# Eight pairs of activation tiles at eight different byte offsets from the weights, modulo 256

## The chip, the core and the metric

The kernel runs on one core of one Trainium2 chip. The metric is the time of one execution on the device, in microseconds (us); the median of the runs shown is compared. TensorE (PE in the profile) does the matrix products, VectorE (DVE), ScalarE (ACT) and GpSimd (POOL) the rest. PEld is TensorE's load of the stationary operand, which the profile lists apart from the matmul that uses it. SP and ACT issue the transfers from memory.

## What is computed

Two layers over x of 512 tokens and 1024 channels, in float32. Each normalises, projects, mixes and projects back onto a residual:

```python
def pool_mixer(h, w_in, w_grp, scale, w_out):
    v, gate = jnp.split(h @ w_in, 2, axis=-1)                 # 1024 -> 2 x 2048
    p = multiscale_pool(v)                                    # trailing means minus the token
    m = jnp.einsum('btgc,gcd->btgd', p, w_grp).reshape(B, T, D_INNER) * scale
    return (m * jax.nn.silu(gate)) @ w_out

def hgrn2_mixer(h, w_in, lb, norm_g, w_out):
    q, fz, i, gate = jnp.split(h @ w_in, 4, axis=-1)          # 1024 -> 4 x 2048
    ...                                                       # gated recurrence in chunks -> o
    return (o * jax.nn.silu(gate)) @ w_out

def reference(x, ...):
    h = x
    h = h + pool_mixer(rms_norm(h, norm_g[0]), ...)
    h = h + hgrn2_mixer(rms_norm(h, norm_g[1]), ...)
    return rms_norm(h, final_g)
```

## The kernel before

**Products in three passes.** A float32 operand is split into a high part and the rest, both of the type fp32r, by `split` (lines 93 to 95; ScalarE casts the high part on line 94, VectorE subtracts on line 95). `mm3` (lines 125 to 128) makes each 128 x 128 by 128 x 512 product from three matmuls: high weights with high activations (line 126), high with low (127), low with high (128). In `matmul(out, a, b)` the operand a is stationary (128 columns are loaded into the array) and b is moving (512 columns stream through it). Each of the three matmuls loads its stationary operand afresh.

**What is stationary and what moves.** `piece` (line 97) loads 512 KB of weights into a tile `wraw` and splits it into `whi` and `wlo` (six buffers each); SP issues the loads, 300 places ahead. `scaled_halves` (line 197) writes the eight pairs `xh0, xl0 .. xh7, xl7`, one for each 128 channels of the normalised input, once in each layer. The products are:

- x moving, weights stationary (`project4` and `project`, lines 130 to 149): the values and gates of layer 0, and the forget, query and gate projections of layer 1. 640 products, 1920 matmuls. The loop over the eight pairs k is outside the three matmuls, and in `project4`, the first projection of each layer, outside four outputs as well.
- x stationary, weights moving (`inputs`, line 394): 128 products, 384 matmuls.
- layer 0, `ph`/`pl` and `zh`/`zl` moving, weights stationary (`mixed` and `project_out`): 64 and 128 products, 192 and 384 matmuls.
- layer 1, `z1h`/`z1l` stationary, weights moving (`out_half`, first three groups): 96 products, 288 matmuls; for the last group `zz` (high part in the slot of `kk`, low part in that of `q`): 32 products, 96 matmuls.

Together 3264 matmuls of 512 columns. The other 774 matmul records are short ones of the recurrence, of transposes and of sums.

**Where the tiles lie.** Within a partition, the scratch of the program comes first, then the pools one behind the other in the order of lines 68 to 71 (`const`, `wpool`, `act`, `small`), then the pool of the layer (`l0`, then `l1` in its place). Within a pool, tiles lie in the order of their first creation, each from a multiple of 32 bytes. A tile whose size is a multiple of 256 bytes leaves the phase (the address modulo 256) as it was; the odd sizes move it. By these sizes:

| tiles | phase before | off the weights |
|---|---|---|
| `wraw`, `whi`, `wlo` | 128 | 0 |
| `xh0 .. xl7` (2048 bytes each) | 128 | 0 |
| `ph`, `pl`, `zh`, `zl` (behind two `win` tiles of 2112 bytes) | 0 | 128 |
| `kk`: high part of `zz` (behind `first`, 2 x 32 bytes) | 192 | 64 |
| `q`: low part of `zz` (behind `e`, 2 x 32 bytes more) | 0 | 128 |
| `z1h`, `z1l` (behind `mo` and `ro`, 128 bytes more) | 128 | 0 |

Slices of a weights tile start at multiples of 512 bytes, so the table holds for every slice.

Of the kernel before, what the change touches and what calls it, by code (L numbers as in the profile page):

```python
# [32 lines left out]
F32 = mybir.dt.float32  # L33
# [7 lines left out]
P = 128  # L41
# [3 lines left out]
KD = D // P  # L45
# [5 lines left out]
EPS = 1e-6  # L51
WINDOWS = (2, 4, 8, 16)
RAW, WB = 3, 6
WARM = 10
NORM_AT, SPREAD_AT = (KD - 2, 2), (KD - 1, 1)
AHEAD = 300
# [9 lines left out]
def trunk(ctx: ExitStack, tc: tile.TileContext, xT, par, ident_d, causal_d, mask_d, fg_d, w0_in, w0_grp, w0_out, w1_in, w1_out, out):  # L66
    nc = tc.nc
    const = ctx.enter_context(tc.tile_pool(name="const", bufs=1))
    wpool = ctx.enter_context(tc.tile_pool(name="wpool", bufs=1))
    act = ctx.enter_context(tc.tile_pool(name="act", bufs=1))  # L70
# [9 lines left out]
    warm = pa.tile([P, 512], F32, name="a", tag="a", bufs=4)  # L80
    for _ in range(WARM):
        nc.tensor.matmul(warm[:, :P], ones, ones, start=True, stop=True)
# [3 lines left out]
    nc.scalar.dma_start(out=pp, in_=par)  # L86
    ident = const.tile([P, P], F32, name="ident")
    mhalf = const.tile([P, 8], F32, name="mhalf")
    nc.gpsimd.memset(mhalf, -0.5)

    h = [const.tile([P, T], F32, name=f"h{k}") for k in range(KD)]
# [99 lines left out]
    def spread_sbuf(rn):  # L191
# [2 lines left out]
        nc.scalar.copy(out=rb, in_=spread(rn))  # L194
        return rb

    def scaled_halves(k, col):
        g = pp[:, col + k:col + k + 1]
        hi = act.tile([P, T], F32R, name=f"xh{k}", tag=f"xh{k}", bufs=1)
        lo = act.tile([P, T], F32R, name=f"xl{k}", tag=f"xl{k}", bufs=1)  # L200
        nc.scalar.activation(out=hi, in_=h[k], func=AF.Copy, scale=g)
        nc.vector.scalar_tensor_tensor(out=lo, in0=h[k], scalar=g, in1=hi, op0=ALU.mult, op1=ALU.subtract)
        return hi, lo
# [13 lines left out]
    with tc.tile_pool(name="l0", bufs=1) as l0:  # L217
        xs, pieces = [], []
        wv = w0_in.rearrange("(k p) n -> p k n", p=P)
        for i in range(4):  # L220
            raw = wpool.tile([P, 2, GC], F32, name="wraw", tag="wraw", bufs=RAW)
            hi = wpool.tile([P, 2, GC], F32R, name="whi", tag="whi", bufs=WB)
            lo = wpool.tile([P, 2, GC], F32R, name="wlo", tag="wlo", bufs=WB)
            for j in range(2):
                k = 2 * i + j
                nc.sync.dma_start(out=h[k], in_=xT[k * P:(k + 1) * P, :])
                nc.sync.dma_start(out=raw[:, j], in_=wv[:, k, 0:GC])
                xs.append(scaled_halves(k, C_NG0))
                split(raw[:, j], hi[:, j], lo[:, j])
                pieces.append((hi[:, j], lo[:, j]))  # L230
# [90 lines left out]
    def hgrn(ctx, general):  # L321
# [6 lines left out]
        for a in Ads:  # L328
            nc.gpsimd.memset(a, 0.0)

        xs = [scaled_halves(k, C_NG1) for k in range(KD)]
        accs, rn, rb = project4(load_in(w1_in, DI), xs, lambda: rms(f"l1{name}", h))

# [447 lines left out]
```

## Time and profile before

| | |
|---|---|
| median of 2 runs | 842.99 us (842.31 to 843.68) |
| the profiled execution: its own time | 843.0 us |
| the profiled execution: span from first to last instruction | 841.2 us |
| PE busy | 826.4 us, 98% of the span |
| DVE, ACT, POOL busy | 550.9, 275.2, 160.6 us |
| mean DMA rate | 94 GB/s |

The profile gives for each engine the time in which an instruction of it was under way. Successive matmuls overlap in it: each is listed for about 0.39 us, and the next starts long before that is over. So neither the busy share nor the listed duration tells how fast the products go; the distance from the start of one matmul to the start of the next does, and the timeline gives the starts.

### The profile page before, as it was taken

To read this page: it belongs to the slowest core of one execution; us is meant where nothing else is said; L and a number is where in the kernel's file an instruction comes from. 1 tells how busy PE (TensorE), PEld (TensorE's weight loads), DVE (VectorE), ACT (ScalarE), POOL (GpSimd) and SP (SyncE) were. 2 spreads that over 40 slices of the span, in tenths; PEclk is the share of its full clock that TensorE was granted. 3 is DMA by queue.
4 is the path that set the end of the run, shared out by engine and by line. 5 is a ranking of instruction groups with operands and counts; after the bars stand their busy time and mean duration, and the time that the engine had idled before them with its cause. 6 is when DMAs were issued, how large, how long until landed. Compare 5 with 4: busy or idle time off the path is not lost.

```text
span 841.2 us, 10459 instructions
## 1 busy us (share of the span) xinstructions
PE 826.4 (98%) x4038; PEld 684.8 (81%) x4038; DVE 550.9 (65%) x837; ACT 275.2 (33%) x474; POOL 160.6 (19%) x204
## 2 busy tenths in 40 slices
PE   9899999999999999999999999999999999999995
PEld 7688888888888888888888888888888888888884
DVE  7766645753686456699269974459974459973744
ACT  7342224213323145323433240433240433242311
POOL 4020001001002013071223300213300213302100
PEclk9999999999999999999999999999999999999998
DMA  6622323122422245223032240332240333230202
GB/s 218 213 75 77 100 101 101 53 98 101 150 82 97 75 151 175 76 76 125 1 101 79 71 141 10 101 101 87 80 135 1 101 101 92 82 128 1 101 13 91
DMA packets 37194, 79.06 MB, mean 94 GB/s; under 512 B 2832, under 2 KB 3088, under 8 KB 37136
## 3 DMA queue, kind: packets, MB, share of 16 engines
q1 hardware_dynamic: 34688, 74.46, 27.1%
q10 hardware_dynamic: 2448, 3.86, 1.3%
q8 instruction: 33, 0.54, 0.3%
q14 instruction: 25, 0.20, 0.1%
HBM read 74.11 MB, written 4.19 MB: 93 GB/s over the span
## 4 chain that ended last, share of the span: by engine, by line
PE 95%; DVE 1%; DMA 1%; ACT 1%; issue 0%; POOL 0%; SPq 0%; POOLq 0%; DVEq 0%; ACTq 0%
PE mm L126 29%; PE mm L127 29%; PE mm L128 29%; PE a L556 2%; PE a L594 2%; PE a L574 1%; PE a L596 1%; PE a L563 1%; DMA wraw<-in_w0i 1%; PE a L438 1%; DVE wlo L95 1%; DMA h<-in_xT 0%; PE a L342 0%; ACT whi L94 0%; PE a L188 0%
## 5 line engine op out<-in xcount | busy, mean ns | idle before, releaser
L126 PE MATMUL mm<-xh,whi 128*128 128x512 f32 x640 | 251.2, 393 | 1.3 <-ACT whi L94 0.7
L128 PE MATMUL mm<-xh,wlo 128*128 128x512 f32 x640 | 249.7, 391 | 1.0 <-DVE wlo L95 1.0
L127 PE MATMUL mm<-xl,whi 128*128 128x512 f32 x640 | 249.7, 390 | 0.0
L94 ACT CAST whi<-wraw 128x1024 fp32r<-128x1024 f32 (+1 forms) x140 | 141.9, 1025 | 252.3 <-PE mm L127 115.5
L95 DVE TENSOR_TENSOR wlo<-wraw,whi 128x1024 fp32r<-128x1024 f32 (+1 forms) x140 | 172.7, 1261 | 57.6 <-ACT whi L94 56.6
L126 PEld LDWEIGHTS mm<-xh,whi 128*128 128x128 f32 x640 | 120.6, 188 | 27.1 <-ACT whi L94 1.4
L128 PEld LDWEIGHTS mm<-xh,wlo 128*128 128x128 f32 x640 | 120.4, 188 | 27.2 <-DVE wlo L95 2.0
L127 PEld LDWEIGHTS mm<-xl,whi 128*128 128x128 f32 x640 | 120.5, 188 | 24.5
L541 DVE RECIPROCAL r<-r 128x512 f32<-128x512 f32 x16 | 53.4, 3340 | 1.5 <-POOL r L540 1.5
L128 PE MATMUL mm<-zh,wlo 128*128 128x512 f32 x128 | 50.6, 395 | 0.0
L126 PE MATMUL mm<-zh,whi 128*128 128x512 f32 x128 | 50.6, 395 | 0.0
L127 PE MATMUL mm<-zl,whi 128*128 128x512 f32 x128 | 50.5, 395 | 0.0
L126 PE MATMUL mm<-whi,xh 128*128 128x512 f32 x128 | 50.1, 391 | 0.0
L128 PE MATMUL mm<-whi,xl 128*128 128x512 f32 x128 | 49.9, 390 | 0.0
L127 PE MATMUL mm<-wlo,xh 128*128 128x512 f32 x128 | 49.9, 390 | 0.0
L351 DVE TENSOR_TENSOR ht<-mm,ht 128x512 f32<-128x512 f32 x32 | 22.1, 689 | 35.5 <-PE mm L128 35.5
L214 DVE TENSOR_TENSOR h<-mm,h 128x512 f32<-128x512 f32 x32 | 22.0, 689 | 32.4 <-PE mm L128 32.3
L414 POOL TENSOR_TENSOR gs<-fz,s 128x512 f32<-128x512 f32 x16 | 21.4, 1336 | 98.6 <-ACT s L412 98.6
L272 POOL TENSOR_TENSOR gs<-gt,sg 128x512 f32<-128x512 f32 x16 | 21.3, 1330 | 92.4 <-ACT sg L270 92.3
L126 PE MATMUL mm<-whi,z1h 128*128 128x512 f32 x96 | 37.6, 392 | 0.0
L128 PE MATMUL mm<-whi,z1l 128*128 128x512 f32 x96 | 37.4, 389 | 0.0
L127 PE MATMUL mm<-wlo,z1h 128*128 128x512 f32 x96 | 37.4, 389 | 0.0
(141 smaller groups left out, 1164.9 us busy)
## 6 DMA issues: line engine op xcount, KB each, us to landing
wraw<-in_w1i SPq DMA_DIRECT2D x64, 512.0 KB, 3.9
wraw<-in_w0i SPq DMA_DIRECT2D x28, 512.0 KB, 4.2
wraw<-in_w0o SPq DMA_DIRECT2D x16, 512.0 KB, 3.9
wraw<-in_w1o SPq DMA_DIRECT2D x16, 512.0 KB, 4.3
wraw<-in_w0g SPq DMA_DIRECT2D x8, 512.0 KB, 4.1
h<-in_xT SPq DMA_DIRECT2D x8, 256.0 KB, 5.0
wraw<-in_w0i SPq DMA_DIRECT2D x8, 256.0 KB, 5.2
hmid<-h ACTq DMA_DIRECT2D x8, 256.0 KB, 2.3
```

Source lines behind the costliest of these rows:

```text
L94: nc.scalar.copy(out=hi, in_=src)
L95: nc.vector.tensor_tensor(out=lo, in0=src, in1=hi, op=ALU.subtract)
L126: nc.tensor.matmul(out, lh, rh, start=start, stop=False)
L127: nc.tensor.matmul(out, lh, rl, start=False, stop=False)
L128: nc.tensor.matmul(out, ll, rh, start=False, stop=stop)
L214: nc.vector.tensor_tensor(out=h[n], in0=acc, in1=h[n], op=ALU.add)
L272: nc.gpsimd.tensor_tensor(out=gs, in0=gt, in1=sg, op=ALU.mult)
L351: nc.vector.tensor_tensor(out=ht[b][:, c], in0=acc, in1=ht[b][:, c], op=ALU.add)
L414: nc.gpsimd.tensor_tensor(out=gs, in0=gt, in1=sg, op=ALU.mult)
L541: nc.vector.reciprocal(out=r, in_=r)
L556: nc.tensor.matmul(a[0:64, b], k[:, c:m], q[:, c:c + P], start=True, stop=True)
L594: nc.tensor.matmul(o[:, b], Ads[pr][:, j, t], v[:, b, n * P:(n + 1) * P], start=True, stop=b == 0)
```

## The change

No instruction is added or removed. `PAD` adds a tile of 128 bytes to the pool `const`, behind `mhalf`. `scaled_halves` creates, the first time it is called for each k below 7, a tile `step{k}` of 8 floats (32 bytes) behind the pair, which nothing reads or writes. The scratch of the program, which lies first, shrinks by 512 bytes.

```diff
+PAD = 32
...
     mhalf = const.tile([P, 8], F32, name="mhalf")
+    const.tile([P, PAD], F32, name="pad")
...
+    staggered = set()
+
     def scaled_halves(k, col):
         g = pp[:, col + k:col + k + 1]
         hi = act.tile([P, T], F32R, name=f"xh{k}", tag=f"xh{k}", bufs=1)
         lo = act.tile([P, T], F32R, name=f"xl{k}", tag=f"xl{k}", bufs=1)
+        if k < KD - 1 and k not in staggered:
+            staggered.add(k)
+            act.tile([P, 8], F32, name=f"step{k}")
...
-    nc = bacc.Bacc("TRN2", target_bir_lowering=False, num_devices=1, dynamic_dma_scratch_size=1024)
+    nc = bacc.Bacc("TRN2", target_bir_lowering=False, num_devices=1, dynamic_dma_scratch_size=512)
```

## Rows read from the trace of the kernel before

**Rows 1.** Page: the span, and PE's busy time, share and instructions.

```profile
span 841.2 us, 10459 instructions
...
PE 826.4 (98%) x4038; PEld 684.8 (81%) x4038; DVE 550.9 (65%) x837; ACT 275.2 (33%) x474; POOL 160.6 (19%) x204
```

**Rows 2.** Page: the chain that ended last, shares by engine.

```profile
PE 95%; DVE 1%; DMA 1%; ACT 1%; issue 0%; POOL 0%; SPq 0%; POOLq 0%; DVEq 0%; ACTq 0%
```

**Rows 3.** PE's waits, first and last of five: us in total, times, longest.

```profile
PE a L188 <- POOL rn_l L180: 2.1, 1, 2.1
...
PE mm L126 <- DVE v L242: 0.5, 1, 0.5
```

**Rows 4.** Two stretches: width; PE, PEld, DVE, ACT, POOL busy (x); PEclk; DMA share, GB/s.

```profile
36.00:150.00 114.00, 113.94 (x497) 93.31 (x498) 70.46 (x97) 36.87 (x46) 12.10 (x22) 1.00 0.30 97
...
400.00:800.00 400.00, 400.00 (x2110) 336.40 (x2109) 268.92 (x437) 129.25 (x276) 90.11 (x96) 1.00 0.25 80
```

**Rows 5.** Matmul groups by line: out<-moving,stationary, shapes, count | busy us, mean ns | idle.

```profile
L127 PE MATMUL mm<-xl,whi 128*128 128x512 f32 x640 | 249.7, 390 | 0.0
...
L128 PE MATMUL mm<-zh,wlo 128*128 128x512 f32 x128 | 50.6, 395 | 0.0
...
L127 PE MATMUL mm<-wlo,xh 128*128 128x512 f32 x128 | 49.9, 390 | 0.0
...
L128 PE MATMUL mm<-ph,wlo 128*128 128x512 f32 x64 | 25.3, 395 | 0.0
...
L594 PE MATMUL a<-vn,Ad 128*128 128x128 f32 x128 | 22.1, 275 | 0.0
...
L126 PE MATMUL mm<-whi,zz 128*128 128x512 f32 x32 | 12.9, 402 | 0.0
L128 PE MATMUL mm<-whi,zz 128*128 128x512 f32 x32 | 12.6, 392 | 0.0
...
L574 PE MATMUL a<-vn,kt 128*128 128x128 f32 x96 | 11.4, 275 | 0.0
```

**Rows 6.** Timeline, x moving: start us, us, engine, line, operation; 42 matmuls apart.

```profile
150.36 0.39 PE L126 MATMUL mm<-xh,whi 128*128 128x512 f32 x1
150.36 0.19 PEld L127 LDWEIGHTS mm<-xl,whi 128*128 128x128 f32 x1
...
159.88 0.39 PE L126 MATMUL mm<-xh,whi 128*128 128x512 f32 x1
```

**Rows 7.** Timeline, p moving (first to last 22 matmuls), z moving (26).

```profile
60.73 0.40 PE L126 MATMUL mm<-ph,whi 128*128 128x512 f32 x1
60.97 0.39 PE L127 MATMUL mm<-pl,whi 128*128 128x512 f32 x1
...
65.86 0.40 PE L127 MATMUL mm<-pl,whi 128*128 128x512 f32 x1
...
95.80 0.39 PE L126 MATMUL mm<-zh,whi 128*128 128x512 f32 x1
...
101.87 0.39 PE L128 MATMUL mm<-zh,wlo 128*128 128x512 f32 x1
```

**Rows 8.** Timeline, weights moving: 26 matmuls apart (x stationary), 23 (z1 stationary).

```profile
378.98 0.39 PE L128 MATMUL mm<-whi,xl 128*128 128x512 f32 x1
...
384.88 0.39 PE L127 MATMUL mm<-wlo,xh 128*128 128x512 f32 x1
...
509.72 0.39 PE L126 MATMUL mm<-whi,z1h 128*128 128x512 f32 x1
...
514.93 0.39 PE L128 MATMUL mm<-whi,z1l 128*128 128x512 f32 x1
```

**Rows 9.** Timeline, weights moving, zz stationary: 27 matmuls apart.

```profile
824.73 0.40 PE L126 MATMUL mm<-whi,zz 128*128 128x512 f32 x1
...
830.97 0.40 PE L126 MATMUL mm<-whi,zz 128*128 128x512 f32 x1
```

**Rows 10.** DMA issues, costliest row: queue, count, KB each, median us to landing.

```profile
wraw<-in_w1i SPq DMA_DIRECT2D x64, 512.0 KB, 3.9
```

## The prediction

> **What bounds the kernel now.** Read the page's busy time first: PE is busy for 826.4 of the 841.2 us of the span [rows 1], and the chain that ended last runs over PE for 95% [rows 2]. Then PE's waits: five groups, 5.3 us together, the longest 2.1 us, at the sum of the first norm [rows 3]. In the stretches from 36 to 150 us and from 400 to 800 us PE is busy all the time at a granted clock of 1.00, which is the level of 2.4 GHz, while VectorE has some third of each stretch free and ScalarE two thirds [rows 4]. So from 36 us to the tail the time is the number of matmuls times the distance between their starts, and this distance is what the change can move.
>
> The listed durations hide that distance, since matmuls overlap, so go to the timeline. With x moving, 42 starts take 159.88 - 150.36 = 9.52 us: 226.7 ns each [rows 6]. With x or z1 stationary and the weights moving it is 5.90 / 26 = 226.9 ns and 5.21 / 23 = 226.5 ns [rows 8]. With p or z moving it is 5.13 / 22 = 233.2 and 6.07 / 26 = 233.5 ns, on average 233.3 [rows 7]; with zz stationary 6.24 / 27 = 231.1 ns [rows 9]. Same shape, same type, same clock, nothing waited for: the groups differ in where their operands lie. The mean durations say the same, 390 ns in the fast groups, 395 with p and z, 402 and 392 for two of the three zz passes [rows 5]. By the table of phases, the groups at 226.7 have both operands at the same phase modulo 256, p and z are 128 bytes off the weights, zz has its high part 64 and its low part 128 off. The load of the next stationary operand is the partner: it begins in the same hundredth of a microsecond as the running matmul and lasts 0.19 us of the 0.227 [rows 6], so two read streams run side by side, and their relative phase costs 4 to 7 ns of each matmul. This is a reading of rows that differ in other ways too (other pools, other sources), so it gets a rival.
>
> **The change part by part.** By the sizes of the tiles: scratch -512 and `pad` +128 put the weights and `xh0` at phase 0 (128 before), still equal. The steps put pair k at 32k off the weights, so pair 0 alone stays equal. All tiles behind `act` move by -512 + 128 + 224 = -160 bytes, that is by -32 against the weights modulo 256: p and z go from 128 off to 96, z1 from 0 to 224 (32 away on the circle), the two parts of zz from 64 and 128 to 32 and 96.
>
> Price of an offset. Known: 0 off costs 226.7 ns, 128 off 233.3, a mixture of 64 (two loads in three) and 128 (one) 231.1. Not known: the odd multiples of 32, and which side of the circle matters. The lower bound is the equal phase, 226.7, since no group of rows is faster; the upper bound is the longest step that the timeline of the slow groups prints, 240 ns from 60.73 to 60.97 us [rows 7] (the others there print as 0.22 to 0.24; 233.3 is their average). For any phase off zero I take the mean of the two slow groups, (233.3 + 231.1) / 2 = 232.2 ns, 5.5 above the equal phase: these two groups are the only rows with an offset, and they lie close together.
>
> - A, x pairs. 1920 matmuls with x moving and 384 with x stationary; the 96 of the first projection start before 36 us behind loads and splits, where a few ns are hidden by the waits for these. Of the remaining 2208, seven pairs in eight are shifted: 1932 x 5.5 ns = +10.6 us. Bounds: 0 and 1932 x 13.3 = +25.7 us.
> - B, z1: 288 x 5.5 = +1.6 us. Bounds: 0 and +3.8.
> - C, p and z: 576 matmuls, from 233.3 to 232.2: -0.6 us. Bounds: -3.8 (equal to the fast groups) and +3.9.
> - D, zz: 96 x (232.2 - 231.1) = +0.1 us.
> - The 774 short records: the tiles of the recurrence move together, so that their offsets among themselves stay. A pass with its operands 128 apart (`vn` with `Ad`) lasts 275 ns, one with equal phases (`vn` with `kt`) 275 ns too [rows 5]: 0.
> - `pad` and the steps are no instructions. The scratch is not used by a load, as SP issues the loads of the weights [rows 10]. Their target goes from phase 128 to 0; should it change the 3.9 us to landing, 300 places of look-ahead hide it, as PE waits for none of these transfers after 36 us [rows 3, 4]. Without that cover, a late load would come to PE as a wait for the high part on line 94. The same holds for operations of VectorE and ScalarE on shifted tiles.
>
> Sum: 10.6 + 1.6 - 0.6 + 0.1 = +11.7 us on the span of 841.2: 852.9. The profiled execution took 843.0, 1.8 more than its span, and the median is 842.99; so 854.7 us, 1.4% more.
>
> A rule that speaks against any effect: the Trainium skill, "TensorE: Matmul & The Clock Gate", Part 2, gives TensorE two independent read ports on SBUF, one for the moving operand and one for the weights, and says that loading the next weights takes nothing from the running matmul. By it the sum would be 0. The 233.3 beside 226.7 ns [rows 6, 7] disagree, if it is the phase that separates them.
>
> **The rivals.**
>
> 1. Starts off a multiple of 64 cost more. No row has an operand at an odd multiple of 32; after the change half the x pairs, z1, p, z and zz do. If those pay the upper 240 ns and even multiples 232.2: 1104 x 13.3 + 828 x 5.5 + 288 x 13.3 + 576 x 6.7 + 96 x 8.9 ns = 14.7 + 4.6 + 3.8 + 3.9 + 0.9 = +27.9, 870.9 us. It decides from a smaller price: slower by 2% is +16.9 us, reached when all shifted matmuls average about 234 ns (2220 x 7.4 + 576 x 0.8 ns). For it: one step in two with p and z is already above 234. Against it: their average is not.
> 2. Phase does not matter; p, z and zz are slower for another reason, such as the place of their tiles or what else is read then. All terms are 0: 843.0 us. For it: the rows with an offset all have tiles of their own. Against it: zz has the same moving weights as z1, in the same stage of the kernel, 226.5 against 231.1 ns [rows 8, 9], with nothing but the stationary tiles' place between them. The rule of the Trainium skill named above is on this rival's side.
> 3. The spread helps: an equal phase is itself a collision, since both streams start together on the same phase, and some offsets lie under it. With as much below as 128 lies above, 220.1 ns: 2220 x -6.6 + 576 x -13.2 + 96 x -11.0 ns = -23.3, 819.7 us. It is faster by 2% from an average of about 222 ns on. Against it: all three offsets that rows show are slower than equal, and the change visits two of them again (64 and 128, pairs 2 and 4). The same page of the Trainium skill (Part 1) gives about 216 ns between starts of 512 columns at full clock; 226.7 ns is 11 above, so there would be room, but no row here comes near it.
>
> **How the numbers follow.** The forecast, 851 to 860 us (shifted matmuls at 230.5 to 234 ns), gets 0.62; rival 1, 860 to 872, gets 0.22; rival 2, and prices near its own, 839 to 848, 0.12; rival 3, 0.04. The predicted time is that of the forecast, 854.7. The range from 845 to 864 holds the forecast, about a third of rival 1 and half of rival 2: some 0.8. A measurement of this kernel tells about 2% from no change, 826 and 860 us: faster 0.04, same 0.70 (the forecast but for its upper edge, and rival 2), slower 0.26 (rival 1 and that edge). The forecast's own sign is slower, inside the 2%.
>
> **What the profile after would show.** The timeline with x moving no longer has one step but eight, in groups of three matmuls for each k: 226.7 ns for k = 0, about 233 for k = 4, and the others between 230 and 234. In the first projection of layer 1 there are twelve in a row for each k. z1 rises from 226.5 to about 232; p and z stay within 2 ns of 233. PE stays busy at a clock of 1.00 from 36 to 800 us with no new wait, and the span grows by as much as the sum of the steps. Rival 1 shows as odd k at 238 to 240; rival 2 as all k at 226.7; rival 3 as steps under 226. The prediction is wrong if an offset of 32 costs more than one of 128, if the phase acts modulo something smaller than 256 (pair 4 would be at 226.7), or if a shifted tile slows ScalarE or VectorE enough to make PE wait.

## The result and the profile after

The changed kernel takes 856.97 us (median of 2 runs, 856.75 to 857.19) against 842.99: a ratio of 1.0164, 95% interval 1.0146 to 1.0181. That is 2.3 us above the predicted 854.7, inside the range of 845 to 864, and slower by less than 2%, as forecast. The page of the profiled execution:

```profile
span 855.3 us, 10459 instructions
...
PE 841.6 (98%) x4038; PEld 686.9 (80%) x4038; DVE 551.8 (65%) x837; ACT 275.2 (32%) x474; POOL 161.6 (19%) x204
...
PE 95%; DVE 2%; DMA 1%; ACT 0%; issue 0%; SPq 0%; POOL 0%; POOLq 0%; DVEq 0%; ACTq 0%
```

The instructions are the same 10459, the chain runs over PE for 95% as in [rows 2], and the span has grown by 14.1 us from [rows 1], of which PE's busy time shows 15.2. The waits of PE (us in total, times, longest), and in the second block the two stretches of [rows 4] (width; busy time and count of PE, PEld, DVE, ACT, POOL; clock; DMA):

```profile
PE a L190 <- POOL rn_l L182: 3.1, 1, 3.1
PE a L83 <- POOL ones L79: 1.0, 1, 1.0
PE mm L130 <- DMA wraw<-in_w0i: 0.2, 1, 0.2
```

```profile
36.00:150.00 114.00, 114.00 (x490) 91.94 (x489) 67.39 (x94) 36.82 (x45) 11.79 (x22) 1.00 0.28 92
400.00:800.00 400.00, 400.00 (x2100) 330.30 (x2101) 263.99 (x435) 126.53 (x272) 88.82 (x95) 1.00 0.24 78
```

No wait is new in the steady part, PE is busy all of it at a granted clock of 1.00, and still it gets through fewer matmuls: 490 instead of 497 and 2100 instead of 2110 [rows 4]. The loss is in the distance between starts. The groups by operation (their lines have moved by two; count, busy us, mean ns, idle) show where:

```profile
L129 PE MATMUL mm<-xl,whi 128*128 128x512 f32 x640 | 252.5, 395 | 0.0
...
L129 PE MATMUL mm<-wlo,xh 128*128 128x512 f32 x128 | 50.3, 393 | 0.0
L130 PE MATMUL mm<-zh,wlo 128*128 128x512 f32 x128 | 50.2, 392 | 0.0
...
L129 PE MATMUL mm<-wlo,z1h 128*128 128x512 f32 x96 | 37.9, 395 | 0.0
...
L601 PE MATMUL a<-vn,Ad 128*128 128x128 f32 x128 | 22.1, 275 | 0.0
```

The x groups have gone from 390 to 395 and 393 ns, while the short passes keep their 275 [rows 5]. The timeline of the changed kernel gives the distances. First z moving (28 matmuls apart); then x moving, from the first matmul of pair 3 to the same of the next product, 24 matmuls on, with the three matmuls of pair 0 and the first of pair 1 between; then z1 stationary (27) and zz stationary (34):

```profile
96.80 0.40 PE L129 MATMUL mm<-zl,whi 128*128 128x512 f32 x1
...
103.33 0.39 PE L130 MATMUL mm<-zh,wlo 128*128 128x512 f32 x1
...
150.39 0.40 PE L128 MATMUL mm<-xh,whi 128*128 128x512 f32 x1
...
153.88 0.40 PE L128 MATMUL mm<-xh,whi 128*128 128x512 f32 x1
154.12 0.39 PE L129 MATMUL mm<-xl,whi 128*128 128x512 f32 x1
154.34 0.39 PE L130 MATMUL mm<-xh,wlo 128*128 128x512 f32 x1
154.57 0.40 PE L128 MATMUL mm<-xh,whi 128*128 128x512 f32 x1
...
155.97 0.40 PE L128 MATMUL mm<-xh,whi 128*128 128x512 f32 x1
...
517.65 0.40 PE L129 MATMUL mm<-wlo,z1h 128*128 128x512 f32 x1
...
523.96 0.39 PE L129 MATMUL mm<-wlo,z1h 128*128 128x512 f32 x1
...
837.62 0.40 PE L129 MATMUL mm<-wlo,zz 128*128 128x512 f32 x1
...
845.51 0.39 PE L130 MATMUL mm<-whi,zz 128*128 128x512 f32 x1
```

A product with x moving takes 5.58 / 24 = 232.5 ns a matmul, 226.7 before [rows 6]; z still 6.53 / 28 = 233.2 [rows 7]; z1 6.31 / 27 = 233.7, 226.5 before [rows 8]; zz 7.89 / 34 = 232.1, 231.1 before [rows 9]. Pair 0, which still lies at the weights' phase, takes (154.57 - 153.88) / 3 = 230 ns, and not 226.7.

From all starts of each group in the two traces (distances over 260 ns, which hold a wait or another kind of matmul, left out), the mean distances are:

| group | before, ns | after, ns | matmuls | worth, us |
|---|---|---|---|---|
| x moving | 226.9 | 232.5 | 1824 | 10.2 |
| x stationary | 227.1 | 231.5 | 384 | 1.7 |
| z1 stationary | 227.0 | 233.3 | 288 | 1.8 |
| p, z moving | 233.2 | 233.3 | 576 | 0.1 |
| zz stationary | 231.1 | 232.2 | 96 | 0.1 |

Together 13.9 of the 14.1 us. And by pair, x moving, after: 231.5 ns for pair 0, 231.5, 232.9, 233.7, 233.3, 234.3, 231.5 and 231.5 for pairs 1 to 7 (32 to 224 bytes off). Before, pair 0 is at 227.6.

In the first projection of layer 1 each pair has twelve matmuls in a row. There pair 0 takes 2.79 / 12 = 232 ns (first line to the first of pair 1), so it is slow even where no other pair comes between:

```profile
327.19 0.39 PE L128 MATMUL mm<-xh,whi 128*128 128x512 f32 x1
...
329.98 0.40 PE L128 MATMUL mm<-xh,whi 128*128 128x512 f32 x1
```

In the same stretch pair 2 (64 off) takes 228.8 and pair 4 (128 off) 233.3 ns.

### The profile page after: what moved, and what is told of

Same layout as the page of the kernel before. It is cut to its first block, busy times and chain, and to the rows that moved or that the text cites. A ratio compares the mean times of both kernels' runs of the same rounds, so it can differ in the third digit from the quotient of the medians.

```text
span 855.3 us, 10459 instructions
## 1 busy us (share of the span) xinstructions
PE 841.6 (98%) x4038; PEld 686.9 (80%) x4038; DVE 551.8 (65%) x837; ACT 275.2 (32%) x474; POOL 161.6 (19%) x204
## 4 chain that ended last, share of the span: by engine, by line
PE 95%; DVE 2%; DMA 1%; ACT 0%; issue 0%; SPq 0%; POOL 0%; POOLq 0%; DVEq 0%; ACTq 0%
PE mm L128 29%; PE mm L129 29%; PE mm L130 29%; PE a L563 2%; PE a L601 2%; PE a L581 1%; PE a L603 1%; PE a L570 1%; DMA wraw<-in_w0i 1%; PE a L445 1%; DVE wlo L97 1%; DMA h<-in_xT 1%; DVE xl L209 0%; PE a L349 0%; PE a L190 0%
## 5 line engine op out<-in xcount | busy, mean ns | idle before, releaser
L128 PE MATMUL mm<-xh,whi 128*128 128x512 f32 x640 | 255.2, 399 | 0.0
L130 PE MATMUL mm<-xh,wlo 128*128 128x512 f32 x640 | 253.6, 397 | 0.2 <-DMA wraw<-in_w0i 0.2
L129 PE MATMUL mm<-xl,whi 128*128 128x512 f32 x640 | 252.5, 395 | 0.0
```

The source lines that it names most:

```text
L128: nc.tensor.matmul(out, lh, rh, start=start, stop=False)
L129: nc.tensor.matmul(out, lh, rl, start=False, stop=False)
L130: nc.tensor.matmul(out, ll, rh, start=False, stop=stop)
```

## Experiments

The theory is that of the prediction: the phase of the moving operand against the stationary one that is being loaded sets the distance between starts. The addresses themselves are in no record; the offsets are worked out from the sizes of the tiles. The rivals are another property of the tiles (their place, their absolute phase) and a special price of odd multiples of 32 bytes. All experiments start from the kernel before, with the scratch at 512 bytes, which leaves every phase as it was.

### The pad alone

```diff
     mhalf = const.tile([P, 8], F32, name="mhalf")
+    const.tile([P, PAD], F32, name="pad")
```

> The pad of 128 bytes and the smaller scratch alone: every tile behind mhalf moves from its phase to the one 128 bytes on, and all offsets between operands stay as before. Theory (the offset between the moving operand and the next weights sets the step): 843 us, x moving at 226.7 ns, p and z at 233.3. Rival (the absolute phase of an operand matters, 128 being the good one before): the fast and the slow groups change places, x at 233 and p and z at 227, 854 us.

Measured: 842.93 us, ratio 0.9995 (0.9986 to 1.0004). Timeline, z moving (27 matmuls apart) and x moving (43):

```profile
96.67 0.40 PE L130 MATMUL mm<-zh,wlo 128*128 128x512 f32 x1
...
102.97 0.39 PE L130 MATMUL mm<-zh,wlo 128*128 128x512 f32 x1
...
150.10 0.39 PE L128 MATMUL mm<-xh,whi 128*128 128x512 f32 x1
...
159.85 0.39 PE L129 MATMUL mm<-xl,whi 128*128 128x512 f32 x1
```

6.30 / 27 = 233.3 and 9.75 / 43 = 226.7 ns, as before, with every operand at another absolute phase. So the absolute phase falls as a cause, which leaves the offset between operands, and the pad and the scratch show no cost.

### The steps between the pairs alone

```diff
+    ahead, behind, seen = {}, {0: 32, 1: 32, 2: 32, 3: 32, 4: 32, 5: 32, 6: 32, 7: 32}, set()
+
     def scaled_halves(k, col):
         g = pp[:, col + k:col + k + 1]
+        if k not in seen and k in ahead:
+            act.tile([P, ahead[k] // 4], F32, name=f"ahead{k}")
         hi = act.tile([P, T], F32R, name=f"xh{k}", tag=f"xh{k}", bufs=1)
         lo = act.tile([P, T], F32R, name=f"xl{k}", tag=f"xl{k}", bufs=1)
+        if k not in seen and k in behind:
+            act.tile([P, behind[k] // 4], F32, name=f"behind{k}")
+        seen.add(k)
```

> The eight pairs lie 0, 32 .. 224 bytes off the weights as in the change, but a step behind the last pair too, so that everything behind them keeps its phase, and no pad. Theory: the x pairs carry nearly all of the loss; z1 back at 226.7 ns saves 288 x 6.6 = 1.9 us of the change's 14.0, so 855 us. Rival (the tiles behind the pairs, or the pad, carry it): under 848 us.

Measured: 854.70 us, ratio 1.0133 (1.0118 to 1.0149), 11.3 us above the 843.39 of the kernel before in the same runs. Timeline, x moving (24 matmuls apart) and z1 stationary (27):

```profile
150.41 0.39 PE L126 MATMUL mm<-xh,whi 128*128 128x512 f32 x1
...
155.99 0.39 PE L126 MATMUL mm<-xh,whi 128*128 128x512 f32 x1
...
514.32 0.39 PE L126 MATMUL mm<-whi,z1h 128*128 128x512 f32 x1
...
520.44 0.39 PE L126 MATMUL mm<-whi,z1h 128*128 128x512 f32 x1
```

That is 5.58 / 24 = 232.5 and 6.12 / 27 = 226.7 ns; over all starts x moving is at 232.6 ns and x stationary at 231.5, as in the change, and z1 back at 227.0. The eight steps put z1 256 bytes further from the weights than in the kernel before, and it is as fast: 256 bytes of offset count as none. The pairs carry four fifths of the change's loss; of the other 2.7 us, z1 accounts for 1.8 and p and z, at 232.4 ns here, for 0.5.

### All pairs 128 bytes off

The same edit with other bytes ahead of and behind the pairs:

```diff
+    ahead, behind, seen = {0: 128}, {7: 128}, set()
```

> All eight pairs 128 bytes off the weights, everything else at its phase of before. Theory: x moving and x stationary step as p and z did, 229 and 238 ns in turn, 233.3 on average; 2208 x 6.6 ns = 14.6, so 857.6 us. Rival (p and z are slow for their place or their stage): 843 us, x at 226.7 ns.

Measured: 855.84 us, ratio 1.0150 (1.0131 to 1.0169). Timeline, x moving, 42 matmuls apart:

```profile
150.11 0.40 PE L126 MATMUL mm<-xh,whi 128*128 128x512 f32 x1
...
159.87 0.40 PE L126 MATMUL mm<-xh,whi 128*128 128x512 f32 x1
```

9.76 / 42 = 232.4 ns. The same products, in the same place of the program, become as slow as p and z by 128 bytes of address. The rival that place or stage alone makes p and z slow falls. The loss is 12.5 us and not 14.6, as x stays at 232.5 ns on average and does not reach 233.3 and the alternation of 229 and 238 ns that was expected does not show in these products.

### All operands at equal phase

```diff
     with tc.tile_pool(name="l0", bufs=1) as l0:
+        l0.tile([P, 32], F32, name="even")
...
         low, rest = lb[:, 4], lb[:, 5]
+        if not general:
+            for tag, shape in (("first", [P, 2, TB]), ("e", [P, 2, TB]), ("mo", [P, TB]), ("ro", [P, TB, 1])):
+                for _ in range(2):
+                    l1.tile(shape, F32, name=tag, tag=tag, bufs=2)
```

> The opposite of the change: a tile of 128 bytes at the head of layer 0's pool, and first, e, mo and ro created at the head of layer 1's, so that p, z and both parts of zz lie at the weights' phase as x and z1 do. Theory: p and z go from 233.3 to 226.7 ns, 576 x 6.6 = 3.8 us, zz from 231.1, 0.4 us: 838.8 us. Rival (place, not phase): 843 us, p and z at 233.3.

Measured: 839.22 us, ratio 0.9946 (0.9932 to 0.9959): 4.2 us faster than the kernel before in the same runs, and the fastest of all kernels here. Timeline, z moving (27 matmuls apart) and zz stationary (33):

```profile
96.82 0.39 PE L126 MATMUL mm<-zh,whi 128*128 128x512 f32 x1
...
102.94 0.39 PE L126 MATMUL mm<-zh,whi 128*128 128x512 f32 x1
...
820.11 0.39 PE L128 MATMUL mm<-whi,zz 128*128 128x512 f32 x1
...
827.59 0.39 PE L128 MATMUL mm<-whi,zz 128*128 128x512 f32 x1
```

6.12 / 27 = 226.7 and 7.48 / 33 = 226.7 ns: p, z and zz were slow for their offset alone, [rows 7] and [rows 9] become [rows 6].

### All pairs 32, 64 and 96 bytes off

```diff
+    ahead, behind, seen = {0: 32}, {7: 224}, set()
...
+    ahead, behind, seen = {0: 64}, {7: 192}, set()
...
+    ahead, behind, seen = {0: 96}, {7: 160}, set()
```

> All eight pairs 32 bytes off the weights, the rest as before; x moving shows 32 off, x stationary 224 off (32 the other way round). Theory that any offset costs about the same: 232 to 234 ns, 855 to 858 us. Theory that the cost grows with the distance on the circle of 256 bytes: 228.4 ns, 847 us. Theory that an odd multiple of 32 costs extra: 238 ns or more, 868 us.

> All eight pairs 64 bytes off; x stationary shows 192 off. Any offset alike: 232 to 234 ns, 855 to 858 us. Growing with the distance: 230 ns, 850 us. An odd multiple of 32 costs extra: as any offset alike, since 64 is an even one.

> All eight pairs 96 bytes off; x stationary shows 160 off. Any offset alike: 232 to 234 ns, 855 to 858 us. Growing with the distance: 231.7 ns, 854 us. An odd multiple of 32 costs extra: 238 ns or more, 868 us.

Measured: 857.73, 849.40 and 858.38 us, ratios 1.0172 (1.0150 to 1.0194), 1.0073 (1.0053 to 1.0093) and 1.0180 (1.0160 to 1.0200). Timelines, for 32 bytes x moving (42 matmuls apart) and x stationary (43):

```profile
150.04 0.39 PE L128 MATMUL mm<-xh,wlo 128*128 128x512 f32 x1
...
159.84 0.39 PE L128 MATMUL mm<-xh,wlo 128*128 128x512 f32 x1
...
383.74 0.40 PE L126 MATMUL mm<-whi,xh 128*128 128x512 f32 x1
...
393.77 0.40 PE L127 MATMUL mm<-wlo,xh 128*128 128x512 f32 x1
```

for 64 bytes (43 and 38):

```profile
149.94 0.39 PE L128 MATMUL mm<-xh,wlo 128*128 128x512 f32 x1
...
159.78 0.39 PE L126 MATMUL mm<-xh,whi 128*128 128x512 f32 x1
...
383.68 0.40 PE L126 MATMUL mm<-whi,xh 128*128 128x512 f32 x1
...
392.55 0.40 PE L128 MATMUL mm<-whi,xl 128*128 128x512 f32 x1
```

and for 96 bytes x moving (42):

```profile
150.13 0.39 PE L128 MATMUL mm<-xh,wlo 128*128 128x512 f32 x1
...
159.93 0.39 PE L128 MATMUL mm<-xh,wlo 128*128 128x512 f32 x1
```

So 233.3 ns at 32 (9.80 / 42), 228.8 at 64 (9.84 / 43), 233.3 at 96; with x stationary, which turns the offset round, 233.3 at 224 (10.03 / 43), 233.4 at 192 (8.87 / 38), and, as the mean over all starts, 234.2 at 160. Odd multiples of 32 do not cost the 238 ns of the rival: the dearest offset is 160, with 234.2, and 32 and 96 cost what 128 costs p and z before (233.3), though 0.8 ns more than 128 costs x (232.5). No offset is faster than none. "Any offset alike" holds but for 64 with x moving, which is the one cheap offset, while 192, as far off on the other side, costs the full price. The growth with the distance is refuted by 32.

### One pair off

```diff
+    ahead, behind, seen = {4: 128}, {4: 128}, set()
```

> Pair 4 alone 128 bytes off the weights, seven pairs at their phase. In the changed kernel pair 0, at equal phase, steps at 231.5 ns and not at 226.7. Theory that each matmul pays for its own offset alone: only three matmuls of 24 at 233, the others at 226.7, 2208 / 8 x 6 ns = 1.7 us, 845 us. Theory that a change of offset costs the matmuls behind it as well, until the step has settled (3 to 6 matmuls at 228 to 236 ns after every interruption in the rows of before): pairs 5 and perhaps 6 at 228 to 232 too, 846 to 848 us.

Measured: 847.23 us, ratio 1.0043 (1.0026 to 1.0059), 3.9 us above the 843.30 of the kernel before in the same runs. Timeline, x moving: the first matmuls of pairs 4, 5, 6 and 7 (three matmuls apart), and of pair 4 of the next product, 15 matmuls after pair 7:

```profile
150.16 0.40 PE L126 MATMUL mm<-xh,whi 128*128 128x512 f32 x1
...
150.86 0.39 PE L126 MATMUL mm<-xh,whi 128*128 128x512 f32 x1
...
151.55 0.40 PE L126 MATMUL mm<-xh,whi 128*128 128x512 f32 x1
...
152.24 0.39 PE L126 MATMUL mm<-xh,whi 128*128 128x512 f32 x1
...
155.64 0.40 PE L126 MATMUL mm<-xh,whi 128*128 128x512 f32 x1
```

Pair 4 takes 0.70 / 3 = 233 ns a matmul, and pairs 5 and 6, at equal phase, take 0.69 / 3 = 230 as well; from pair 7 on it is 3.40 / 15 = 226.7. Means over all starts: 234.0, 224.8 and 237.1 for the three matmuls of pair 4, then 229.9, 235.2, 228.5, 232.3, 230.6, and 226.7 from the sixth on. Above 226.7 that is 16 ns in a product for the pair itself and 23 for the five matmuls behind it; 39 ns x 2208 / 24 = 3.6 of the 3.9 us. So here an offset costs those behind it more than itself.

How long this lasts is not fixed. In the first projection of layer 1, pair 5 has twelve matmuls in a row behind the twelve of pair 4:

```profile
338.45 0.39 PE L126 MATMUL mm<-xh,whi 128*128 128x512 f32 x1
...
341.18 0.39 PE L126 MATMUL mm<-xh,whi 128*128 128x512 f32 x1
```

They take 2.73 / 12 = 228 ns, and are at 226.7 from the fourth on. In the kernel before, at equal phase, up to eight matmuls at 224 to 236 ns follow an interruption, more than the three to six of the expectation. But the twelve of pair 0 in the changed kernel, at 232 ns, do not settle at all.

## Why the prediction held, and where it did not

- **What bounds the kernel**: right. No new wait, the clock at 1.00, and 13.9 of 14.1 us from the distances between starts.
- **Phase as the cause**: argued from rows that differed in other ways, and shown by the runs: 128 bytes ahead of x make it slow, 128 ahead of p and z make these fast, and 128 ahead of everything change nothing. Rival 2 falls: 232.4 against 226.7 ns by the offset between the two operands alone. The rule of the Trainium skill beside it ("TensorE: Matmul & The Clock Gate", Part 2: two independent read ports, and a load that takes nothing from the running matmul) does not agree, and the measurement decides. That it is the two reads that meet is still argued, from the load that begins with the running matmul [rows 6]: no run took the load away.
- **Term A**, +10.6 us: measured 10.2 + 1.7 = 11.9. The step that failed is that pair 0, since it alone stays equal, keeps 226.7 ns. It is at 231.5, against 227.6 before, and carries 1.0 us that A put at nothing; the seven shifted pairs carry 10.9. What slows pair 0 is shown in part: in the products its three matmuls stand behind pair 7's, and the run with one pair shows that matmuls at equal phase pay behind an offset one, there the first five. But in the first projection twelve were not enough either, and why they do not settle stays open. The price of 232.2 ns for the shifted pairs was near the measured 231.5 to 234.3, and that is partly luck: the mean of two rows hit it by their likeness, not by a law. Alone, an offset of 64 costs 229.0 ns and the others 232.5 to 234.2, while pair 2, 64 off, takes 232.9 among the others. The upper bound of 240 ns was the difference of two rounded starts; the longest step there is 238.
- **Term B**, +1.6: measured 1.8. **Term C**, -0.6: measured +0.1, as 96 off costs what 128 off does. **Term D**, +0.1, and the short records, 0: as measured. Of the 2.3 us between 854.7 and the result, A has 1.3, C 0.7 and B 0.2.
- **Edits at no cost**: right, the pad and the smaller scratch are 0.9995 of the time before.
- **Rival 1** (odd multiples of 32): refuted at its price of 240 ns by 233.3 at 32 and at 96, the price of 128 with p and z. The prediction's sign of being wrong, 32 dearer than 128, is too close to call: 32 is 0.8 ns above x at 128, level with p and z, and these vary as much at one offset (232.4 to 233.3). **Rival 3** (some offset is faster): refuted for all seven offsets tried uniformly. Offsets under 32 bytes were not tried.
- **What the profile would show**: pairs between 230 and 234 ns, z1 at about 232 (233.3) and p, z within 2 ns of 233 came out; k = 0 did not.

## To carry to other kernels

Where matmuls follow each other without a wait and still take longer than others of their shape, compare the distances of their starts, not the listed durations, and then the addresses of their operands: here, in fp32r, operands at equal phase modulo 256 were 1 to 3% faster a matmul, and small tiles ahead in the pool, of sizes that are no multiple of 256 bytes, decided it. Fill them up to one; equal phases for all operands gave 0.5% here. Keep all operands of a run of matmuls at one phase, since one pair at another phase slowed the matmuls behind it too.

## What was not expected of the hardware

- The distances settle at 226.67 ns with equal phases, and at 233.33 on average with x moving 32 and 96 bytes off and with p and z 128 off in the kernel before: as 34 to 35. Offsets of 64 (228.9) and of 128 for x (232.4) settle elsewhere. In the products of the run with one pair off, five matmuls pass before the first value is back.
- p and z, untouched in the runs with the steps alone, with 128 and with 64 bytes, were at 232.4 ns there, and at 233.1 to 233.3 in all other runs at 128 off, with the same offsets. So there is more than one steady pattern at this offset. Each kernel has one trace, so whether the kernel or the execution chooses it stays open, as does why 64 bytes are cheap with x moving and 192 with x stationary are not.
